# Which queue carries the stores of the first stretch: from SyncE's queue to ScalarE's, and in the last head group to GpSimd's

## The chip, the cores and the metric

The kernel runs on one core of one Trainium2 chip. The metric is device microseconds of the whole program. An engine's name is shortened as in the profile: PE is TensorE (matmuls), DVE VectorE, ACT ScalarE, POOL GpSimd, SP SyncE. A DMA is issued by an instruction in the queue of one of SP, ACT and POOL; this instruction stands in order with the engine's other instructions and waits there until its data are ready. The 16 DMA engines then move the bytes.

## The reference

One inference step of a one-layer hybrid decoder, for a prompt of 512 tokens and for 8 samples of one token each that carry states. Only the first part, a combined projection with two recurrent branches, is touched here:

```python
def layer(x, p, conv_prev, ssm_prev, wkv_prev, shift_prev, lp):
    h = rmsnorm(x, lp['norm_mix'])
    z, xbc_raw, dt_raw, rw_proj, gate_m, gate_r = split_proj(h @ lp['w_in'])
    y_m, conv_new, ssm_new = mamba_branch(z, xbc_raw, dt_raw, ...)
    y_r, wkv_new, shift_new = rwkv_branch(rw_proj, shift_prev, wkv_prev, ...)
    x = x + (jax.nn.sigmoid(gate_m) * y_m + jax.nn.sigmoid(gate_r) * y_r) @ lp['w_out']
    x = x + peer(rmsnorm(x, lp['norm_ffn']), ...)
    x = x + jax.nn.sigmoid(rmsnorm(x, lp['norm_ple']) @ lp['w_ple_gate']) * (p @ lp['w_ple_proj'])

def wkv_scan(r, decay, k, v, a_vec, b_vec, s0):          # RWKV-7, 16 heads of 64
    def step(s, inp):
        rt, wt, kt, vt, at, bt = inp
        s = (s * wt[:, :, None, :]
             + jnp.einsum('bhvk,bhk->bhv', s, at)[..., None] * bt[:, :, None, :]
             + vt[..., None] * kt[:, :, None, :])
        return s, jnp.einsum('bhvk,bhk->bhv', s, rt)
...
    def step(h, inp):                                    # Mamba-2 SSD, 32 heads, in chunks of 128
        st, dec = inp
        return h * dec[..., None, None] + st, h
```

The model width is 1024, everything is fp32. The outputs are the final activations and the new states of prompt and samples.

## The kernel before

The first stretch (about 34 to 1230 us of the span) works through 8 head groups in a loop `for g in range(8)`; a group is two RWKV heads and four SSD heads. Every 128 columns of `w_in` are one projection tile: the weights are loaded by SP's queue (L86, `wraw`, two buffers), split by ACT (L78, `whi`) and DVE (L79, `wlo`) into a high and a low part, and multiplied in three passes (L95, L96, L97), 24 matmuls of 260 columns for each half of the 520 tokens. These matmuls need nothing of the group that is in work, so they can fill PE's time wherever they stand in its order. Below they are called fills.

For a group the steps are: `rwkv_in` (L513 to L567 prepare the chunks' factors), `rwkv_inv` (the inverse of 16x16 blocks: 15 steps on DVE, L598 and L601, an ACT copy L602, then a round trip through DRAM to re-lay the result: a store of `td` L603, a load by ACT's queue L606, then L610 on DVE into `di` and on POOL into `dp`), `rwkv_pre` (PE L513, L645, L655, L665 with DVE L632, L634, L636, L647 and POOL L671), and `rwkv_chain`: 8 dependent steps, each PE L703, DVE L707, PE L711, ACT L712 and L713, PE L717, DVE L723 and L726, and every four of them PE L737 and L735; it ends with PE L743. Then `rwkv_out` (L752 to L762) and `ssd` (L952 to L1019). `gates()` makes the 16 tiles of the two branch gates, each stored by L1065; in the code's order three tiles stand ahead of the last group's chain and 13 behind it.

The 8 samples' recurrent steps run as generators one group behind the prompt: `rwkv_s` (store L814 of five rows to `q5_d`, six broadcast loads L823, the state's load L828, DVE L830 to L836 with POOL L832 and L833, the state's store L837) and `ssd_s` (store L891 to `bc_d`, loads L905 and L906, then twice a state's load L910, POOL L912, DVE L913 and L914, the state's store L915, POOL L916). The last group's own sample steps run beside its chain.

The functions don't fix the order in which an engine takes its instructions. A scheduler at build time picks, from a model of each queue, which of the ready instructions each engine takes next; only those in `pin(...)` keep the order of the code. A changed queue therefore moves other instructions too. Once built, each engine's order is fixed.

Of the kernel before, what the change touches and what calls it, by code (L numbers as in the profile page):

```python
# [18 lines left out]
P = 128  # L19
# [11 lines left out]
def tile_hybrid(ctx: ExitStack, tc, x_prompt, x_sample, p_prompt, p_sample, state_ssm, state_conv,  # L31
# [6 lines left out]
    nc = tc.nc  # L38
    V, S, G, T = nc.vector, nc.scalar, nc.gpsimd, nc.tensor
# [8 lines left out]
    def rowb(ap, n):  # L48
        return ap.unsqueeze(0).to_broadcast([n] + list(ap.shape))
# [20 lines left out]
    bc_d = dram.tile([8, 8, 256], F32, name="bc_d")  # L70
    g_d = dram.tile([2, 8, P, 2, NH], F32, name="g_d")
# [502 lines left out]
    def rwkv_inv(g, ar, bk):  # L574

        L64 = c8(full("de"))
        lc16 = lp.tile([P, 8, 16], F32, name="lw")
        for hf in range(2):
            hs = slice(4 * hf, 4 * hf + 4)
            L = mm4(lambda ro, i: ar[ro, 4 * hf + i, 0, :], lambda ro, i: bk[ro, 4 * hf + i, ro.start // 64, :])  # L580
            V.tensor_tensor(L64[:, hs], L, b64(m64, 4), op=OP.mult)
            lm = c8(full("kk"))[:, 0:4]
            V.tensor_tensor(lm, L, b64(m16, 4), op=OP.mult)
            V.tensor_reduce(lc16[:, hs], lm.rearrange("p c (b k) -> p c k b", k=16), axis=AX.X, op=OP.add)
        ld, td = ld_d[g % 2], td_d[g % 2]
        nc.scalar.dma_start(ld.rearrange("c p k -> p c k"), lc16)
        yield
        lb = lp.tile([64, 16, 16], F32, name="a")
        pin(nc.sync.dma_start(lb.rearrange("q r k -> q (r k)"), ld.rearrange("c (z r) k -> (c z) (r k)", r=16)))
        yield  # L590
        tb = lp.tile([64, 16, 32], F32, name="sq")
        pin(V.memset(tb, 0.0))
        V.memset(tb.rearrange("p r k -> p (r k)")[:, 0:512:33], 1.0)
        tf = lp.tile([64, 16, 16], F32, name="k2")
        for j in range(15):
            tt = tf[:, j + 1:, 0:j + 1]
            sh = [64, 15 - j, j + 1]
            i = V.tensor_tensor(tt, lb[:, j + 1:, j:j + 1].to_broadcast(sh), tb[:, j:j + 1, 0:j + 1].to_broadcast(sh), op=OP.mult)  # L598
            if j == 0:
                pin(i)  # L600
            V.tensor_tensor(tb[:, j + 1:, 0:j + 1], tb[:, j + 1:, 0:j + 1], tt, op=OP.add)  # L601
        S.copy(tb[:, :, 16:32], tb[:, :, 0:16].rearrange("p r k -> p k r"))  # L602
        nc.sync.dma_start(td.rearrange("c (z r) k -> (c z) (r k)", r=16), tb.rearrange("q r k -> q (r k)"))  # L603
        yield
        tc16 = lp.tile([P, 8, 32], F32, name="lw")
        pin(nc.scalar.dma_start(tc16, td.rearrange("c p k -> p c k")))  # L606
        yield
        T16, TT16 = c8(full("di")), c8(full("dp"))
        for q, (E_, t) in enumerate(((V, T16), (G, TT16))):
            pin(E_.tensor_tensor(t.rearrange("p c (b k) -> p c b k", k=16),  # L610
                                 tc16[:, :, None, 16 * q:16 * q + 16].to_broadcast([P, 8, 4, 16]),
                                 mb16[:, None].to_broadcast([P, 8, 4, 16]), op=OP.mult))
        yield L64, T16, TT16
# [135 lines left out]
    def rwkv_out(g, y, bon, lw_):  # L749
# [11 lines left out]
        V.tensor_tensor(y, y, ps, op=OP.mult)  # L761
        nc.sync.dma_start(yr_d[g], y.rearrange("p (i t) -> p i t", i=2))  # L762


    def rwkv_s(g, lw_):
        gs = slice(g * P, (g + 1) * P)
# [44 lines left out]
        T.transpose(ps[:40, 0:P], Q.rearrange("p q b -> p (q b)"), identf)  # L811
        qs = l2.tile([40, P], F32, name="s_qs", bufs=1)
        S.copy(qs, ps[:40, 0:P])
        nc.sync.dma_start(q5_d[g], qs)  # L814
        yield
        sa = t8("sa")

# [2 lines left out]
        qa, qb, qc, w2 = big("sB"), big("sB"), big("sH"), big("sH")  # L820
        for i, (dst, n) in enumerate(((qa, 16), (qb, 16), (qc, 8))):
            for e in range(2):
                m = nc.sync.dma_start(dst[64 * e:64 * e + 64].rearrange("p q b k -> p (q b) k")[:, :n],  # L823
                                      rowb(q5_d[g, 16 * i:16 * i + n, 64 * e:64 * e + 64], 64))
                if i == e == 0:
                    pin(m)
        dec, nkk, bS, kS, rS, sw, t1, t2 = qa[:, 0], qa[:, 1], qb[:, 0], qb[:, 1], qc[:, 0], qc[:, 1], w2[:, 0], w2[:, 1]
        nc.sync.dma_start(sw, state_wkv[0].rearrange("b h v k -> b (h v) k")[:, gs].rearrange("b p k -> p b k"))  # L828
        yield
        pin(V.tensor_tensor(t1, sw, nkk, op=OP.mult))  # L830
        V.tensor_reduce(sa, t1, axis=AX.X, op=OP.add)
# [2 lines left out]
        V.tensor_tensor(t1, bS, bl(sa, 64), op=OP.mult)  # L834
        V.tensor_tensor(sw, sw, t1, op=OP.add)
        V.tensor_tensor(sw, sw, t2, op=OP.add)  # L836
        nc.sync.dma_start(wkv_sample[0].rearrange("b h v k -> b (h v) k")[:, gs].rearrange("b p k -> p b k"), sw)  # L837
        G.tensor_tensor(t2, sw, rS, op=OP.mult)
        V.tensor_reduce(yrS[:, g], t2, axis=AX.X, op=OP.add)

# [32 lines left out]
    def ssd_s(g):  # L873
        def pA():
            return pa.tile([P, 512], F32, name="psA")
        js = (2 * g, 2 * g + 1, 16 + g, 24 + g)
        cvv = cvS.rearrange("p c (b k) -> p c b k", k=3)
        xc = l2.tile([P, 4, 8], F32, name="s_xc", bufs=1)
        th = l2.tile([P, 4, 8], F32, name="s_th", bufs=1)
        for i, j in enumerate(js):  # L880
            V.tensor_scalar(xc[:, i], fl8(xbcS)[:, j], cw[:, 3, j:j + 1], rows["conv_b"][:, j:j + 1], op0=OP.mult, op1=OP.add)
            for k in range(3):
                V.scalar_tensor_tensor(xc[:, i], cvv[:, j, :, k], cw[:, k, j:j + 1], xc[:, i], op0=OP.mult, op1=OP.add)
        S.activation(th, xc, AF.Tanh)
        V.scalar_tensor_tensor(xc, th, 1.0, xc, op0=OP.add, op1=OP.mult)
        ps = pA()
        for i in range(2):
            T.transpose(ps[:8, i * P:(i + 1) * P], xc[:, 2 + i], identf)
        bcs = l2.tile([8, 256], F32, name="s_bc", bufs=1)
        S.copy(bcs, ps[:8, 0:256])  # L890
        nc.sync.dma_start(bc_d[g], bcs)  # L891
        ps = pA()
        for i in range(2):
            for e in range(2):
                T.matmul(ps[64 * e:64 * e + 64, i * 16:i * 16 + 16],
                         lhsT=selb[:, 4 * g + 2 * i + e:4 * g + 2 * i + e + 1].to_broadcast([96, 64]), rhs=limbS, start=True, stop=True)
        dx = l2.tile([P, 2, 16], F32, name="s_dx", bufs=1)
        V.tensor_copy(dx, ps[:, 0:32].rearrange("p (j b) -> p j b", b=16))
        V.tensor_tensor(dx[:, :, 0:8], dx[:, :, 0:8], xc[:, 0:2], op=OP.mult)
        sst = state_ssm[0].rearrange("b h p n -> b (h p) n")  # L900
        sso = ssm_sample[0].rearrange("b h p n -> b (h p) n")
        y2 = yS[:, 2 * g:2 * g + 2]
        yield
        Bb, Cb = (lp.tile([P, 8, P], F32, name="sB", bufs=2) for _ in range(2))
        pin(nc.sync.dma_start(Bb, rowb(bc_d[g, :, 0:P], P)))  # L905
        nc.sync.dma_start(Cb, rowb(bc_d[g, :, P:2 * P], P))  # L906
        for i in range(2):
            rs_ = slice(js[i] * P, (js[i] + 1) * P)
            hs_, t1 = (lp.tile([P, 8, P], F32, name="sH", bufs=2) for _ in range(2))
            pin(nc.sync.dma_start(hs_, sst[:, rs_].rearrange("b p n -> p b n")))  # L910
            yield
            pin(G.tensor_tensor(t1, Bb, bl(dx[:, i, 0:8], P), op=OP.mult))  # L912
            pin(V.tensor_tensor(hs_, hs_, bl(dx[:, i, 8:16], P), op=OP.mult))  # L913
            V.tensor_tensor(hs_, hs_, t1, op=OP.add)  # L914
            nc.sync.dma_start(sso[:, rs_].rearrange("b p n -> p b n"), hs_)  # L915
            G.tensor_tensor(t1, hs_, Cb, op=OP.mult)  # L916
            V.tensor_reduce(y2[:, i], t1, axis=AX.X, op=OP.add)
            if i == 0:
                yield
        for i in range(2):  # L920
            V.scalar_tensor_tensor(y2[:, i], xc[:, i], dsk[:, js[i]:js[i] + 1], y2[:, i], op0=OP.mult, op1=OP.add)
        zs = fl8(zS)[:, 2 * g:2 * g + 2]
        t = l2.tile([P, 2, 8], F32, name="s_t2", bufs=1)
        S.activation(t, zs, AF.Tanh, scale=0.5)
        V.scalar_tensor_tensor(t, t, 1.0, zs, op0=OP.add, op1=OP.mult)
        V.tensor_tensor(y2, y2, t, op=OP.mult)
# [11 lines left out]
    def ssd(g, xt, bm, cm, sz):  # L938
# [59 lines left out]
            T.transpose(ps[:, j * P:(j + 1) * P], st[:, j * P:(j + 1) * P], identf)  # L998
        so = l2.tile([P, 2, P], F32, name="yt")
        S.copy(so, ps[:, 0:256].rearrange("p (j n) -> p j n", j=2))  # L1000
        nc.sync.dma_start(ssm_prompt[0, 0].rearrange("h q n -> (h q) n")[g * 256:(g + 1) * 256].rearrange("(j p) n -> p j n", p=P), so)

        for j in range(2):
            G.tensor_tensor(yf[j], yf[j], sz[j], op=OP.mult)
# [54 lines left out]
    def gates():  # L1059
        for i, c0 in enumerate((W_GR, W_GM)):  # L1060
            for o in range(8):
                ps = proj(c0 + o * P, P, hT)
                gt = l2.tile([P, 2, NH], F32, name="dtmp")
                S.activation(gt, ps[:, :, :NH], AF.Tanh, scale=0.5)
                nc.sync.dma_start(g_d[i, o], gt)  # L1065
                step()
                yield
    gates_ = gates()
# [644 lines left out]
```

## Time and profile before

| | us |
|---|---|
| median of 3 runs | 3083.57 (3078.41 to 3088.08) |
| the profiled execution's own time | 3087.78 |
| its span, from the first to the last instruction | 3086.1 |
| PE busy | 2819.7 (91%) |
| DVE busy | 2268.4 (74%) |
| ACT busy | 988.0 (32%) |
| POOL busy | 679.2 (22%) |
| mean granted PE clock | 0.944 of full speed |

The rows of the next sections come from the profiled execution; start times are microseconds from the beginning of its span. It is 4.2 us (0.14%) longer than the median run. The span holds the first stretch to about 1230 us, the output projections and keys to about 1580 us, and the PEER passes and the end behind them.

### The profile page before, as it was taken

How to read it: one execution, taken by the hardware profiler on the slowest of the kernel's cores; microseconds unless marked ns; L12 is line 12 of the kernel's file. 1: busy time of each engine (PE TensorE's matmuls, PEld its weight loads, DVE VectorE, ACT ScalarE, POOL GpSimd, SP SyncE). 2: the span in 40 equal slices, each digit the busy share in tenths (PEclk: the TensorE clock that was granted, in tenths of full speed). 3: DMA queues.
4: the chain of work that ended last, by engine and by line, in shares of the span. 5: the costliest groups of instructions: out<-in, count | busy, mean ns of one | idle time of the engine just before them, and what ended most of it. 6: DMA issues, size and time to landing. Idle time of an engine off the chain costs nothing. (4 is left out here: it accounts for less than half of the span.)

```text
span 3086.1 us, 52530 instructions
## 1 busy us (share of the span) xinstructions
PE 2819.7 (91%) x20187; PEld 2617.2 (85%) x20192; DVE 2268.4 (74%) x5375; ACT 988.0 (32%) x1995; POOL 679.2 (22%) x508
## 2 busy tenths in 40 slices
PE   5999989898897988998987989898999999999998
PEld 4878878787776878896976989898999999999996
DVE  5768787877777684435899999695677777877846
ACT  2333333333241322322222324233222343333322
POOL 0222131212313121210003132121222323432300
PEclk8999999898988898999998999999999999999999
DMA  3214242433324264633224767677898888999830
GB/s 92 71 41 105 78 114 57 105 62 100 82 69 107 61 139 145 203 98 129 76 75 156 240 216 235 218 245 234 299 330 310 321 300 311 332 327 321 290 124 28
DMA packets 459091, 528.15 MB, mean 171 GB/s; under 512 B 102632, under 2 KB 370555, under 8 KB 458801
## 3 DMA queue, kind: packets, MB, share of 16 engines
q1 hardware_dynamic: 405337, 388.99, 41.4%
q0 software_dynamic: 36864, 134.23, 12.6%
q10 hardware_dynamic: 16640, 1.57, 0.4%
q8 instruction: 159, 2.61, 0.4%
q14 instruction: 91, 0.75, 0.1%
HBM read 447.83 MB, written 77.14 MB: 170 GB/s over the span
## 5 line engine op out<-in xcount | busy, mean ns | idle before, releaser
L96 PE MATMUL ps<-hlo,whi 128*128 128x260 f32 (+1 forms) x1456 | 444.0, 305 | 0.0
L97 PE MATMUL ps<-hhi,wlo 128*128 128x260 f32 (+1 forms) x1456 | 443.1, 304 | 0.1
L95 PE MATMUL ps<-hhi,whi 128*128 128x260 f32 (+1 forms) x1456 | 442.2, 304 | 0.3 <-ACT hhi L155 0.3
L97 PE MATMUL psA<-h2h,ul 128*128 128x392 f32 x1024 | 352.9, 345 | 27.4 <-DVE ul L1496 26.9
L95 PE MATMUL psA<-h2h,uh 128*128 128x392 f32 x1024 | 364.2, 356 | 0.2 <-ACT uh L1495 0.2
L95 PE MATMUL av<-ah,vh 128*128 128x392 f32 x1024 | 349.9, 342 | 3.8 <-ACT vh L78 3.2
L96 PE MATMUL psA<-h2l,uh 128*128 128x392 f32 x1024 | 353.3, 345 | 0.0
L97 PE MATMUL av<-ah,vl 128*128 128x392 f32 x1024 | 351.8, 344 | 1.3 <-DVE vl L79 1.3
L96 PE MATMUL av<-al,vh 128*128 128x392 f32 x1024 | 350.5, 342 | 2.3 <-DVE al L79 2.3
L97 PEld LDWEIGHTS ps<-hhi,wlo 128*128 128x128 f32 (+1 forms) x1456 | 286.4, 197 | 11.9 <-issue 5.9
L95 PEld LDWEIGHTS ps<-hhi,whi 128*128 128x128 f32 (+1 forms) x1456 | 286.3, 197 | 12.0 <-issue 5.5
L96 PEld LDWEIGHTS ps<-hlo,whi 128*128 128x128 f32 (+1 forms) x1456 | 286.9, 197 | 10.3 <-issue 4.4
L1449 POOL DMA_INDIRECT gr<-in_peer_v_dram,e x128 | 194.8, 1522 | 363.8 <-DVE o L1464 346.4
L1449 POOL DMA_INDIRECT gr<-in_peer_u_dram,e x128 | 127.4, 995 | 498.1 <-DVE junk L1458 452.1
L78 ACT CAST vh<-vr 128x1024 fp32r<-128x1024 f32 x128 | 134.3, 1051 | 315.8 <-PE av L96 155.1
L97 PEld LDWEIGHTS psA<-h2h,ul 128*128 128x128 f32 x1024 | 195.7, 191 | 30.9 <-DVE ul L1496 29.7
L78 ACT CAST whi<-wraw 128x1024 fp32r<-128x1024 f32 (+1 forms) x115 | 119.9, 1042 | 313.8 <-PE ps L96 247.9
L95 PEld LDWEIGHTS av<-ah,vh 128*128 128x128 f32 x1024 | 193.5, 189 | 4.8 <-ACT vh L78 3.5
L95 PEld LDWEIGHTS psA<-h2h,uh 128*128 128x128 f32 x1024 | 195.6, 191 | 0.9 <-ACT uh L1495 0.9
L96 PEld LDWEIGHTS psA<-h2l,uh 128*128 128x128 f32 x1024 | 196.3, 192 | 0.0
L96 PEld LDWEIGHTS av<-al,vh 128*128 128x128 f32 x1024 | 193.2, 189 | 3.1 <-DVE al L79 3.1
L97 PEld LDWEIGHTS av<-ah,vl 128*128 128x128 f32 x1024 | 193.2, 189 | 1.8 <-DVE vl L79 1.8
(627 smaller groups left out, 6453.0 us busy)
## 6 DMA issues: line engine op xcount, KB each, us to landing
ur<-in_peer_u_dram SPq DMA_DIRECT2D x128, 512.0 KB
vr<-in_peer_v_dram SPq DMA_DIRECT2D x128, 512.0 KB
wraw<-in_w_in_dram SPq DMA_DIRECT2D x90, 512.0 KB
Gt<-G_d SPq DMA_DIRECT2D x32, 784.0 KB
G_d<-stg SPq DMA_DIRECT2D x12, 2048.0 KB
ge_d<-ge SPq DMA_DIRECT2D x112, 196.0 KB
gl<-ge_d SPq DMA_DIRECT2D x112, 196.0 KB
sB<-q_d SPq DMA_DIRECT2D x32, 256.0 KB
```

Source lines behind the costliest of these rows:

```text
L78: S.copy(hi, raw)
L95: T.matmul(out, lhsT=a[0], rhs=b[0], start=start, stop=False)
L96: T.matmul(out, lhsT=a[0], rhs=b[1], start=False, stop=False)
L97: T.matmul(out, lhsT=a[1], rhs=b[0], start=False, stop=stop)
L1449: pin(G.indirect_dma_start(out=t, out_offset=None, in_=(peer_u, peer_v)[s_ // P][0], in_offset=bass.IndirectOffsetOnAxis(ap=e3[:, s_ % P:s ...
```

## The change

Two groups of DMA instructions are issued by another engine; what they move, and where the code stands, is the same.

- In all groups, the stores of what ACT made are issued by ACT and no longer by SP: L603 (`td`), L814 (`q5_d`), L891 (`bc_d`), L1001 (the prompt's SSD state, an output) once in each of 8 groups, and L1065 (`g_d`) 16 times, 48 DMAs.
- A helper `Qu(g)` gives POOL's queue for the last group (g == 7) and SP's otherwise. Through it go the samples' loads and state stores: six L823, L828, L837, L905, L906, two L910 and two L915, so 14 DMAs of the last group are issued by POOL.

```diff
-        nc.sync.dma_start(td.rearrange("c (z r) k -> (c z) (r k)", r=16), tb.rearrange("q r k -> q (r k)"))
+        nc.scalar.dma_start(td.rearrange("c (z r) k -> (c z) (r k)", r=16), tb.rearrange("q r k -> q (r k)"))
...
+    def Qu(g):
+
+        return G if g == 7 else nc.sync
+
...
-        nc.sync.dma_start(q5_d[g], qs)
+        nc.scalar.dma_start(q5_d[g], qs)
...
-                m = nc.sync.dma_start(dst[64 * e:64 * e + 64].rearrange("p q b k -> p (q b) k")[:, :n],
+                m = Qu(g).dma_start(dst[64 * e:64 * e + 64].rearrange("p q b k -> p (q b) k")[:, :n],
...
-        nc.sync.dma_start(sw, state_wkv[0].rearrange("b h v k -> b (h v) k")[:, gs].rearrange("b p k -> p b k"))
+        Qu(g).dma_start(sw, state_wkv[0].rearrange("b h v k -> b (h v) k")[:, gs].rearrange("b p k -> p b k"))
...
-        nc.sync.dma_start(wkv_sample[0].rearrange("b h v k -> b (h v) k")[:, gs].rearrange("b p k -> p b k"), sw)
+        Qu(g).dma_start(wkv_sample[0].rearrange("b h v k -> b (h v) k")[:, gs].rearrange("b p k -> p b k"), sw)
...
-        nc.sync.dma_start(bc_d[g], bcs)
+        nc.scalar.dma_start(bc_d[g], bcs)
...
-        pin(nc.sync.dma_start(Bb, rowb(bc_d[g, :, 0:P], P)))
-        nc.sync.dma_start(Cb, rowb(bc_d[g, :, P:2 * P], P))
+        pin(Qu(g).dma_start(Bb, rowb(bc_d[g, :, 0:P], P)))
+        Qu(g).dma_start(Cb, rowb(bc_d[g, :, P:2 * P], P))
...
-            pin(nc.sync.dma_start(hs_, sst[:, rs_].rearrange("b p n -> p b n")))
+            pin(Qu(g).dma_start(hs_, sst[:, rs_].rearrange("b p n -> p b n")))
...
-            nc.sync.dma_start(sso[:, rs_].rearrange("b p n -> p b n"), hs_)
+            Qu(g).dma_start(sso[:, rs_].rearrange("b p n -> p b n"), hs_)
...
-        nc.sync.dma_start(ssm_prompt[0, 0].rearrange("h q n -> (h q) n")[g * 256:(g + 1) * 256].rearrange("(j p) n -> p j n", p=P), so)
+        nc.scalar.dma_start(ssm_prompt[0, 0].rearrange("h q n -> (h q) n")[g * 256:(g + 1) * 256].rearrange("(j p) n -> p j n", p=P), so)
...
-                nc.sync.dma_start(g_d[i, o], gt)
+                nc.scalar.dma_start(g_d[i, o], gt)
```

The helper takes four lines, so in the changed kernel each line behind it has a number that is 4 higher: L823 is L827, L830 is L834, L836 is L840, L912 is L916, L916 is L920, and L913 is L917; all text here uses the numbers of before.

The scheduler's order changes with the queues. On PE, this is the second half of the last group's chain before the change (`uv`, `X`, `TT` and `ctok` are the chain's own tiles, x2 the two heads):

```order
L737 MATMUL psB<-AM,uv 64x64 x8
L735 MATMUL psB<-ar,st 64x64 x8
L703 MATMUL psB<-uv,AM 64x64 x2
L711 MATMUL psB<-X,TT_11985 64x64 x2
L717 MATMUL psB<-uv,ctok 64x64 x2
L703 MATMUL psB<-uv,AM 64x64 x2
L711 MATMUL psB<-X,TT_11985 64x64 x2
L717 MATMUL psB<-uv,ctok 64x64 x2
```

The same place on PE after the change (`hhi`, `hlo` are the activations' parts, `whi`, `wlo` the weights' of a gate or projection tile):

```order
L703 MATMUL psB<-uv,AM 64x64 x2
L97 MATMUL ps<-hhi,wlo 128x260
L95 MATMUL ps<-hhi,whi 128x260
L96 MATMUL ps<-hlo,whi 128x260
L97 MATMUL ps<-hhi,wlo 128x260
L95 MATMUL ps<-hhi,whi 128x260
L96 MATMUL ps<-hlo,whi 128x260
L97 MATMUL ps<-hhi,wlo 128x260
L95 MATMUL ps<-hhi,whi 128x260
L711 MATMUL psB<-X,TT_11985 64x64 x2
L96 MATMUL ps<-hlo,whi 128x260
```

Counted over the whole order, the last group's chain (L701 to L743) holds no fill before and 125 after; from L743 to L760 it is 39 and 63, and from there to the end of the gates (PE L845) 345 and 168. 28 fills of the 384 stand ahead of the chain now. In groups 1 to 6 the chain holds 125 to 148 fills before, and 97 to 158 after.

On POOL, this is the last group before the change (L912 and L916 ahead of L671 belong to group 6's samples, all behind to group 7's):

```order
L916 TENSOR_TENSOR sH<-sH,sB 128x1024
L671 COPY AM<-ar 64x4x64 x2
L833 TENSOR_TENSOR sH<-sB,s_x_11923 128x512
L832 TENSOR_TENSOR sH<-sH,sB 128x512
L838 TENSOR_TENSOR sH<-sH 128x512
L912 TENSOR_TENSOR sH<-sB,s_dx 128x1024
```

The same place on POOL after it:

```order
L827 DMA sB<-q_d 64x16x64 x2
L920 TENSOR_TENSOR sH<-sH,sB 128x1024
L671 COPY AM<-ar 64x4x64 x2
L827 DMA sB<-q_d 64x16x64
L671 COPY AM<-ar 64x4x64 x2
L827 DMA sB<-q_d 64x16x64
L827 DMA sH<-q_d 64x8x64 x2
L832 DMA sH<-in_state_wkv_dram 128x8x64
L837 TENSOR_TENSOR sH<-sB,s_x_11923 128x512
L836 TENSOR_TENSOR sH<-sH,sB 128x512
L841 DMA out_dram<-sH 128x8x64
L842 TENSOR_TENSOR sH<-sH 128x512
```

Seven DMAs now stand between POOL's own operations here (the rows x2 count twice, and the first two are ahead of group 6's last L916); the other seven follow behind.

On DVE, this is group 5 before the change, from the samples' state update to the first evictions of `rwkv_pre`; the inverse's last step L601 stands 7 rows ahead of the first row shown:

```order
L836 TENSOR_TENSOR sH<-sH 128x512
L775 TENSOR_TENSOR s_x_9774<-s_x_9774,rwS 128x24
L792 TENSOR_SCALAR s_kx<-s_x_9774,VB 128x8
L804 COPY s_Q<-s_x_9774 128x8
L793 TENSOR_TENSOR s_t<-s_kx 128x8
L839 TENSOR_REDUCE yrS<-sH 128x8
L610 TENSOR_TENSOR di<-lw,mb_270 128x512
L632 TENSOR_TENSOR bb<-psB,di 128x256
L913 TENSOR_TENSOR sH<-sH,s_dx 128x1024
L632 TENSOR_TENSOR a<-psB,di 128x256
```

The same group on DVE after the change, first from the inverse's last step on:

```order
L601 TENSOR_TENSOR sq<-sq,k_8442 64x15
L79 TENSOR_TENSOR wlo<-wraw,whi 128x1024
L610 TENSOR_TENSOR di<-lw,mb_270 128x512
L834 TENSOR_TENSOR sH<-sH,sB 128x512
L835 TENSOR_REDUCE s_sa<-sH 128x8
L838 TENSOR_TENSOR sH<-sB,s_sa 128x512
```

and then, some rows on, around the evictions:

```order
L843 TENSOR_REDUCE yrS<-sH 128x8
L632 TENSOR_TENSOR bb<-psB,di 128x256
L632 TENSOR_TENSOR a<-psB,di 128x256
L634 TENSOR_TENSOR k_8791<-psB,di 128x256
L634 TENSOR_TENSOR sq<-psB,di 128x256
L917 TENSOR_TENSOR sH<-sH,s_dx 128x1024
```

L610 has moved from behind the samples' operations to ahead of them, and L913 from between the two L632 to behind the four evictions; groups 4 and 6 read alike, and L610 has moved so in groups 1, 2 and 7 too (in group 3 it stands behind L830). POOL's L610 keeps its place there, behind the samples' L832, L833 and L838.

## Rows read from the trace of the kernel before

**Rows 1.** Windows: stretch in us, its length, each engine's busy us, PE clock, DMA share, GB/s.

```profile
core 0: us, PE busy (x) PEld busy (x) DVE busy (x) ACT busy (x) POOL busy (x), PEclk, DMA share, GB/s
305.20:335.95 30.75, 30.75 (x318) 25.78 (x316) 20.21 (x58) 11.40 (x33) 7.81 (x5) 1.00 0.35 100
...
1149.81:1177.31 27.50, 15.66 (x170) 10.86 (x170) 15.55 (x57) 6.30 (x24) 3.23 (x5) 0.50 0.50 103
1177.31:1188.07 10.76, 10.28 (x70) 8.39 (x67) 4.86 (x17) 1.26 (x3) 3.16 (x2) 0.87 0.73 200
1188.07:1230.00 41.93, 41.93 (x349) 41.69 (x347) 18.39 (x21) 10.87 (x15) 8.26 (x3) 1.00 0.60 177
34.00:1240.00 1206.00, 1069.92 (x9383) 933.92 (x9388) 885.28 (x2181) 383.96 (x976) 278.52 (x206) 0.90 0.36 89
```

**Rows 2.** The same windows, PE's instructions of L95 alone.

```profile
305.20:335.95 30.75, 13.02 (x43) 8.09 (x43) 1.00 0.35 100
...
1149.81:1177.31 27.50, 0.00 (x0) 0.00 (x0) 0.50 0.50 103
...
1188.07:1230.00 41.93, 32.88 (x115) 21.63 (x115) 1.00 0.60 177
```

**Rows 3.** Timeline of PE in the last group's chain: start, us, instruction, [idle before it <-releaser].

```profile
1168.90 0.48 PE L717 MATMUL psB<-uv,ctok 128*64 128x64 f32 x4 [0.54 <-ACT uv L713]
```

**Rows 4.** Timeline of PE where the gates end.

```profile
1229.90 0.33 PE L845 MATMUL psB<-yrS,bdm 128*128 128x64 f32 x2
```

**Rows 5.** Timeline of DVE where the last group's sample steps end.

```profile
1209.65 0.29 DVE L867 TENSOR_TENSOR yS<-yS,VB 128x128 f32<-128x128 f32 x1
```

**Rows 6.** Waits of PE, 70 to 1240 us: us in total, times, longest.

```profile
PE psB L513 <- POOL dp L610: 17.4, 5, 6.1
```

**Rows 7.** Waits of ACT in the same window.

```profile
ACT whi L78 <- PE ps L96: 174.5, 57, 13.0
```

**Rows 8.** Waits of SP's queue in the same window.

```profile
SPq L603 <- ACT sq L602: 43.1, 7, 7.8
```

**Rows 9.** Groups by line: ns min/median/max of one issue, first and last start.

```profile
L603 SPq DMA_DIRECT2D td_d<-sq x8: 477/484/484, 146.9 to 1111.5; - x8
L814 SPq DMA_DIRECT2D q_d<-s_qs x8: 295/304/313, 257.5 to 1131.6; - x8
L891 SPq DMA_DIRECT2D bc_d<-s_bc x8: 286/298/432, 253.1 to 1161.1; - x8
L1001 SPq DMA_DIRECT2D out_dram<-yt x8: 383/389/1502, 190.2 to 1132.0; - x8
L1065 SPq DMA_DIRECT2D g_d<-dtmp x16: 319/332/532, 1058.5 to 1231.6; - x16
...
L823 SPq DMA_DIRECT2D sB<-q_d x32: 590/934/2524, 259.1 to 1150.7; - x32
...
L1449 POOL DMA_INDIRECT gr<-in_peer_u_dram,e x128: 932/936/1926, 1637.6 to 2348.3; - x128
```

**Rows 10.** Timeline of POOL in the last group.

```profile
1157.02 1.04 POOL L833 TENSOR_TENSOR sH<-sB,s_x 128x512 f32<-128x512 f32 x1 [6.23 <-DMA sB<-q_d]
1174.02 1.26 POOL L832 TENSOR_TENSOR sH<-sH,sB 128x512 f32<-128x512 f32 x1 [15.95 <-DVE sH L830]
```

**Rows 11.** Timeline of SP's queue in the last group.

```profile
1151.62 2.13 SPq L823 DMA_DIRECT2D sH<-q_d  x2
```

**Rows 12.** Timeline of DVE in group 5, behind the inverse.

```profile
834.00 0.68 DVE L830 TENSOR_TENSOR sH<-sH,sB 128x512 f32<-128x512 f32 x1
...
842.19 0.67 DVE L610 TENSOR_TENSOR di<-lw,mb 128x512 f32<-128x512 f32 x1
...
848.81 1.23 DVE L913 TENSOR_TENSOR sH<-sH,s_dx 128x1024 f32<-128x1024 f32 x1 [3.81 <-DMA sH<-in_state_ssm_dram]
```

**Rows 13.** Timeline of POOL in group 5.

```profile
840.39 1.26 POOL L610 TENSOR_TENSOR dp<-lw,mb 128x512 f32<-128x512 f32 x1
```

**Rows 14.** Timeline of PE in group 5, from the inverse to the chain's inputs.

```profile
841.70 1.97 PE L513 MATMUL psB<-dp,de 64*64 64x64 f32 x32 [6.07 <-POOL dp L610]
...
850.42 1.12 PE L513 MATMUL psB<-a 64*64 64x64 f32 x16 [4.39 <-DVE a L632]
...
856.01 2.40 PE L645 MATMUL psB<-ar,bk 64*128 64x128 f32 x16 [2.15 <-DVE TT L636]
```

## The prediction, made before the changed kernel ran

> **What bounds the kernel now.** First the windows over the first stretch: of its 1206 us PE is busy 1069.92, at a mean clock of 0.90, so here the time goes where PE stands idle or runs at the lower of its two levels [rows 1]. The change leaves the order on all engines alone behind the gates, so only this stretch counts. Then the windows of single chains. The chain of group 1 took 30.75 us with PE busy throughout, at full clock, with 43 matmuls of L95, about 129 fills. That of the last group took 27.50 us with none, PE busy 15.66 us at half clock; its 345 fills stand behind it and took 41.93 us, PE busy throughout [rows 1, 2]. The timeline shows why the empty chain is slow: PE waits for ACT and DVE in each step, here 0.54 us ahead of L717 [rows 3]. So the last group pays twice, 11.84 us idle and a half clock, then fills on their own at 41.93/345 = 0.1215 us each. The gates end at 1229.90, the samples' last step at about 1210 [rows 4, 5]: 20 us of slack on the sample side.
>
> Then the lists of waits: is SP, which is relieved, a bound? ACT's cast of a weight tile waits 174.5 us in total for PE to free its buffer [rows 7], so weights lie there early. And SP waits for ACT's copy ahead of L603 in 7 of 8 groups [rows 8], so the store leaves the moment its data are there. A store on ACT can't leave earlier. What could gain, then, isn't the queue itself but the order that the scheduler makes with it.
>
> **The change part by part.**
>
> *48 stores to ACT.* By the medians 8 x 0.484 + 8 x 0.304 + 8 x 0.298 + 8 x 0.389 + 16 x 0.332 = 17.1 us more work for ACT [rows 9]. ACT is busy 383.96 of 1206 us [rows 1], and most stores stand behind the ACT operation that made the data, not ahead of one for which PE waits. Cover is missing in the last chain only, where five of them fall between L712 and L713 of its steps: 5 x 0.33 = 1.6 us. Without cover anywhere it would be 17.1; I take 1.6.
>
> *The last group's order on PE.* Before: 27.50 + 10.76 + 41.93 = 80.2 us from L703's first step to the gates' end [rows 1]. After: the chain holds 125 fills, like group 1's. It takes 30.75 less 4 x 0.12, and 1.6 for ACT's stores, so 31.9. The stretch to L760 has 24 fills more, 10.76 + 24 x 0.1215 = 13.7. The 168 left take 20.4. Together 66.0, so 14.2 less. 28 fills have moved ahead of the chain, where they cost between nothing (if PE waits there anyway) and 28 x 0.1215 = 3.4; I take 2. This term is -12. Bounds: -14 where all of it holds; 0 where the chain stalls at the same places in spite of fills.
>
> *14 DMAs to POOL.* How long POOL is held by issuing a broadcast DMA of 64 partitions is in no row. SP takes 0.934 us for one [rows 9]. POOL's own gathers of 128 rows take 0.932 [rows 9], and L823 has 64 x 16 = 1,024 runs, eight times as many: 0.93 and 8 x 0.93 = 7.4 us are the two ends. I take 1.5 us, near the lower end, since nothing in the rows shows a price per run, and SP's price for the same DMA lies there. What waits behind them: two stand ahead of L916 and four between L671 and L833. POOL starts these four at about 1151, so the load of the state leaves at 1151 + 4t; from SP's last L823 (1151.62) to L833's start was 5.4 us [rows 10, 11]. DVE's L830 then stands ready at 1156.4 + 4t, and in the new order it is ahead of the fifth chain step's L723. That step comes at about 1166 (half of the chain). So up to t = 2.4 it costs nothing; beyond, the whole chain waits 4 us for each us of t. Four more DMAs (L837, L905, L906, the first L910) stand ahead of L913, which stands ahead of part of `rwkv_out` on DVE: again 4 us for each us, from about the same t. So nothing up to t = 2, then 8 us per us. At 1.5 nothing. What POOL computes there took 3.23 us in the chain [rows 1], so it has room. At the end, the samples finish near 1212 at t = 2, the gates at about 1218, so this path is hidden too, but only by some 6 us.
>
> A sentence by the Trainium skill on the same price: "DMA: Bandwidth & Descriptors", section "Anatomy of one DMA — SWDGE (gpsimd) path", states that descriptor generation on this path is small and variable, and that many descriptors can be emitted before it shows; by that t stays near the low end and the sum is the same -12. No run here shows it so far.
>
> *Groups 1 to 6 on DVE.* The sum could fail here. In group 5 the inverse's end was at 834.0; the samples' L830 and its kin ran while the block made its way through DRAM, and DVE's L610 came at 842.19, POOL's at 840.39, right behind POOL's L838 [rows 12, 13]. PE waited 6.07 us for that `dp` [rows 14]; in all groups such waits came to 17.4 us [rows 6]. In the new order DVE's L610 is ahead of the sample operations. It waits for the round trip, at most to 840.4 (POOL's L610 had its data then), and they run behind it. POOL's L610 still stands behind POOL's L838, which needs DVE's L836. So the chain of sample operations, 834.00 to the end of POOL's L610 at 841.65, 7.65 long, starts up to 7 us later: `dp` comes late by 0 (if the round trip is short) to 7 us. I take 5, in groups 4 to 6 and in one of the earlier ones (there, fills have covered such waits so far). On the other side, L913 no longer stands between the two L632. It waited 3.81 us for its state's load, and through it PE waited 4.39 for `a` and then 2.15 for TT [rows 12, 14]; that is 6.5 us per group, in groups 4 to 6. So 4 x 5 - 3 x 6.5 = about 0. Bounds: -20 (no delay, the stalls gone) to +28 (four groups by 7, nothing given back).
>
> **Sum**: -12 + 0 = -12; against the profiled execution (3087.78, span 3086.1) about 3076, against the median of 3083.57, which is 0.14% lower, 3071.6; I say 3071. The forecast's own range is 3058 to 3077, from a few us of middle groups given back or lost.
>
> **The rivals.**
>
> *The middle groups eat it.* `dp` is late by 5 in four groups and the stalls on L632 don't fall away, since DVE is late by as much as L913 was. Then -12 + 20 = +8: 3091; with half of that, 3081. For it: these stalls are in the trace, on PE, with nothing beside them. Against: the evictions come ahead of L913 now, as they did in groups 1 to 3, where PE did not wait so long.
>
> *GpSimd's queue is slow* (the other side). The mechanism: POOL, held t per DMA, feeds L830 and L913 late, and the last chain stands behind them on DVE. It outweighs the 12 us from t = 3.5, is 0.3% slower from t = 4.7, and at 7.4 gives -12 + 43 = +31: 3115. For it: 1,024 runs against the gather's 128 rows. Against: SP issues the same in 0.9.
>
> *The change does nothing.* If a fill only moves from one place to another and the chain's waits stay (each fill delays the chain's next matmul by what it hid), the time is 3083. For it: the fills behind the chain ran dense already. Against: group 1's chain, dense at 30.75 us with 129 fills, where 129 fills alone cost 15.7, so it does overlap. The Trainium skill's "DMA: Bandwidth & Descriptors", section "Issuing engines are not separate DMA queues", speaks for this rival: DMAs of all issuers interleave on the same 16 engines, and issuing on several saves the sequencer's time alone. By that the moved DMAs themselves gain nothing, which agrees with the waits on SP, and it would be 3083 too; the order of PE isn't in the rule.
>
> **How the numbers follow.** 0.3% of the time, 9.25 us, is about what a measurement of this kernel can tell from no change: below 3074.3 is faster, above 3092.8 slower. The forecast has 0.50 (0.47 of it faster), the middle groups 0.23 (0.18 same, 0.05 slower), slow POOL 0.19 (0.14 slower, 0.03 same, 0.02 still faster by its small end), no effect 0.08. So faster 0.49, same 0.32, slower 0.19. The likeliest is 3071. The range of 3050 to 3102 takes in the forecast with the middle groups' gain down to -20 in part, the second and fourth case whole, and slow POOL up to t of about 6; what is left out is 0.05 below and 0.08 above. The forecast's own range, 3058 to 3077, stands beside it since both signs are held.
>
> **What the new profile would show.** Right: in the last chain's window some 42 matmuls of L95, PE busy nearly throughout at a clock near 1.0, some 32 us from L703's first step to L743, and the gates ending about 66 us behind the chain's start. Each DMA row on POOL at 0.9 to 2 us. The waits of PE for `dp` longer than 17.4 us in total, those for `a` at L632 shorter. Wrong: a wait of DVE's L830 or L913 for their loads in the last group, with PE's L703 behind it (POOL slow); PE waits for `dp` of 10 us or more per group with the ones behind it unchanged (middle groups); or a last chain that holds its fills and still lasts 27.5 + 15 us (no effect).

## The result, and the profile after

The changed kernel takes 3057.57 us (median of 6 runs, 3051.57 to 3070.37), the kernel before, beside it, 3087.35 (3078.41 to 3098.93). The ratio is 0.9891, with a 95% interval of 0.9873 to 0.9908: 1.1% or about 34 us faster. The forecast was 12 us and the median lies outside the range of the forecast's own case (3058 to 3077) by a hair; the wide range, 3050 to 3102, holds it, but the gain is nearly three times the one forecast.

In the profiled execution (span 3049.9) the gates end at 1199.78 where they ended at 1229.90 [rows 4], 30.1 us earlier. About half of that lies in the last group, from its chain's start to the gates' end: 80.1 us before, 64.9 now. The other half is gone ahead of it: the last chain starts at 1134.84, where it started at 1149.81. The span is 36.2 us shorter; the other 6 us lie behind the gates, where no order changed, and runs of one kernel differ by more than that. The windows of the last chain and of what is behind it, in the columns of [rows 1]:

```profile
1134.84:1163.41 28.57, 28.44 (x297) 23.25 (x294) 17.65 (x51) 10.04 (x28) 8.33 (x9) 1.00 0.47 119
1163.41:1199.78 36.37, 34.03 (x258) 32.03 (x258) 21.90 (x32) 7.26 (x11) 11.39 (x7) 0.95 0.61 183
34.00:1210.00 1176.00, 1071.33 (x9383) 933.45 (x9387) 864.21 (x2181) 384.92 (x977) 296.83 (x220) 0.92 0.36 91
```

The same chain, PE's instructions of L95 alone, as in [rows 2]:

```profile
1134.84:1163.41 28.57, 12.10 (x41) 7.71 (x41) 1.00 0.47 119
```

The chain took about as long as the empty one (28.57 against 27.50), at full clock and with PE busy throughout, and holds 41 of L95; what is behind it is 16 us shorter. That is the fill that the order showed. Over the stretch to 10 us behind the gates, PE's idle time was 1206 - 1069.92 = 136.1 us before [rows 1] and is 1176 - 1071.33 = 104.7 now, at the same busy time. The equal busy time is a balance of two parts. These are the windows of groups 1 to 3 and of groups 4 to 6, each from a group's first L513 to another's, before:

```profile
229.93:653.34 423.41, 386.30 (x3461) 333.55 (x3464) 336.25 (x803) 150.11 (x391) 105.59 (x78) 0.95 0.36 87
653.34:1075.05 421.71, 364.72 (x3130) 318.47 (x3130) 309.00 (x749) 128.47 (x329) 97.03 (x74) 0.86 0.35 85
```

and after:

```profile
226.07:654.36 428.29, 400.58 (x3462) 344.66 (x3463) 322.58 (x803) 149.67 (x391) 104.60 (x78) 0.93 0.35 86
654.36:1052.87 398.51, 351.30 (x3115) 306.60 (x3115) 297.49 (x747) 129.43 (x329) 105.81 (x73) 0.89 0.36 88
```

Groups 1 to 3 are 4.9 us longer: 9.4 us less idle, but 14.3 more busy, at a lower mean clock (0.93 against 0.95). Groups 4 to 6 are 23.2 us shorter, 9.8 of it idle time and 13.4 busy time, at a higher mean clock (0.89 against 0.86).

The waits of PE, 70 to 1240 us, for the lines of [rows 6]:

```profile
PE psB L513 <- POOL dp L610: 23.2, 6, 6.7
...
PE psB L645 <- DVE TT L636: 3.3, 6, 0.8
...
PE psB L513 <- DVE a L632: 0.2, 1, 0.2
```

The waits for `dp` have grown, from 17.4 to 23.2. Those for `a` at L632 are down to 0.2. In the kernel before, the same list from 600 to 1012 us (groups 4 to 6) had them so:

```profile
PE psB L513 <- POOL dp L610: 16.2, 3, 6.1
PE psB L513 <- DVE a L632: 12.6, 3, 4.4
...
PE psB L645 <- DVE TT L636: 6.4, 3, 2.1
```

Group 5 in the timeline of PE after, from the inverse to the chain's start; the rows answer to [rows 14]:

```profile
837.97 1.97 PE L513 MATMUL psB<-dp,de 64*64 64x64 f32 x32 [6.69 <-POOL dp L610]
...
845.24 1.16 PE L645 MATMUL psB<-ar,bk 64*128 64x128 f32 x8 [0.79 <-DVE TT L636]
...
856.25 0.42 PE L701 MATMUL psB<-uv,AM 64*64 64x64 f32 x4
```

And DVE there, as [rows 12], from the inverse's last step L601 on (L913 is now numbered L917):

```profile
822.06 0.16 DVE L601 TENSOR_TENSOR sq<-sq,k 64x15 f32<-64x15 f32 x1
...
829.68 0.69 DVE L610 TENSOR_TENSOR di<-lw,mb 128x512 f32<-128x512 f32 x1
...
841.70 0.42 DVE L632 TENSOR_TENSOR a<-psB,di 128x256 f32<-128x256 f32 x1 [0.43 <-PE psB L513]
...
843.63 1.22 DVE L917 TENSOR_TENSOR sH<-sH,s_dx 128x1024 f32<-128x1024 f32 x1
```

From `dp`'s L513 to the first L645 it is now 7.3 us, before 14.3 [rows 14]: the state update waits for nothing and stands ahead of none of the four evictions; PE waits 0.79 for the TT behind it. POOL's L610 there, as [rows 13]:

```profile
836.66 1.26 POOL L610 TENSOR_TENSOR dp<-lw,mb 128x512 f32<-128x512 f32 x1
```

And the whole stretch of group 5 from `dp`'s L513 to the chain's start, first before, then after:

```profile
841.70:869.85 28.15, 19.79 (x218) 17.73 (x219) 18.82 (x23) 7.40 (x16) 10.03 (x8) 0.56 0.68 193
837.97:856.25 18.28, 14.71 (x209) 13.22 (x210) 14.22 (x19) 5.44 (x11) 10.01 (x6) 0.69 0.80 225
```

It is 9.9 us shorter: 4.8 of idle time and 5.1 of busy time. Nine fills that stood in it before, 0.22 us apart where fills at full clock are 0.12 apart, are no longer in it (218 matmuls against 209).

POOL's DMAs, as groups by line (L827 is L823 of before):

```profile
L827 POOL DMA_DIRECT2D sB<-q_d x4: 820/852/1071, 1119.5 to 1132.9; - x4
L827 POOL DMA_DIRECT2D sH<-q_d x2: 694/699/704, 1133.7 to 1134.4; - x2
```

0.7 to 1.1 us each, under the 1.5 that the forecast took. The samples' last step on DVE, as [rows 5], comes 7 us ahead of the gates' end:

```profile
1192.78 0.29 DVE L871 TENSOR_TENSOR yS<-yS,VB 128x128 f32<-128x128 f32 x1
```

### The profile page after: what moved, and what is told of

The parts are those of the page before. It is cut to its first block, busy times and chain, and to the rows that moved or that the text cites. A ratio compares the mean times of both kernels' runs of the same rounds, so it can differ in the third digit from the quotient of the medians.

```text
span 3049.9 us, 52517 instructions
## 1 busy us (share of the span) xinstructions
PE 2821.5 (93%) x20188; PEld 2617.4 (86%) x20192; DVE 2249.9 (74%) x5375; ACT 988.6 (32%) x1995; POOL 685.8 (22%) x522
## 2 busy tenths in 40 slices
DMA packets 446995, 528.15 MB, mean 173 GB/s; under 512 B 95464, under 2 KB 357243, under 8 KB 446705
## 5 line engine op out<-in xcount | busy, mean ns | idle before, releaser
L95 PE MATMUL ps<-hhi,whi 128*128 128x260 f32 (+1 forms) x1456 | 443.8, 305 | 0.6 <-DVE rsa L122 0.3
L95 PE MATMUL psA<-h2h,uh 128*128 128x392 f32 x1024 | 365.7, 357 | 0.2 <-ACT uh L1499 0.2
L95 PE MATMUL av<-ah,vh 128*128 128x392 f32 x1024 | 348.9, 341 | 3.3 <-ACT vh L78 3.2
L95 PEld LDWEIGHTS ps<-hhi,whi 128*128 128x128 f32 (+1 forms) x1456 | 286.6, 197 | 13.9 <-issue 6.8
L97 PEld LDWEIGHTS ps<-hhi,wlo 128*128 128x128 f32 (+1 forms) x1456 | 286.3, 197 | 12.6 <-issue 4.0
L1453 POOL DMA_INDIRECT gr<-in_peer_v_dram,e x128 | 184.3, 1440 | 367.9 <-DVE o L1468 349.7
L95 PEld LDWEIGHTS psA<-h2h,uh 128*128 128x128 f32 x1024 | 196.7, 192 | 0.9 <-ACT uh L1499 0.9
L79 DVE TENSOR_TENSOR vl<-vr,vh 128x1024 fp32r<-128x1024 f32 x128 | 156.2, 1222 | 55.4 <-ACT vh L78 52.2
L95 PEld LDWEIGHTS av<-ah,vh 128*128 128x128 f32 x1024 | 192.9, 188 | 3.9 <-ACT vh L78 3.5
```

The source lines that it names most:

```text
L79: eng.tensor_tensor(lo, raw, f(hi), op=OP.subtract)
L95: T.matmul(out, lhsT=a[0], rhs=b[0], start=start, stop=False)
L97: T.matmul(out, lhsT=a[1], rhs=b[0], start=False, stop=stop)
L1453: pin(G.indirect_dma_start(out=t, out_offset=None, in_=(peer_u, peer_v)[s_ // P][0], in_offset=bass.IndirectOffsetOnAxis(ap=e3[:, s_ % P:s ...
```

## The experiments

Two theories stood at the start. One: only the order that the scheduler builds matters, and there are two separate gains, the last chain's fill and the place of L913 and L610 in the middle groups. Rival: SP's queue is relieved, and the gain goes with the DMAs taken off it. All ratios are to the kernel before, run beside.

**Only the gates' stores on ACT** (L1065):

```diff
-                nc.sync.dma_start(g_d[i, o], gt)
+                nc.scalar.dma_start(g_d[i, o], gt)
```

> Only the 16 stores of the gates (L1065) are issued by ACT; everything else as before. In the built order groups 0 to 6 are as before, and the last group's chain holds 127 fills in place of none. Theory (order on PE in the last group, and order in groups 1 to 6, as two separate gains): the last group alone gains, about 15 us, so some 3072 where before is 3087; the chain's window runs at a clock near 1.0 with some 42 of L95, and the waits of PE at L513, L632, L636 in groups 4 to 6 stay. Rival (what gains is SP's relief, in proportion to the DMAs taken off it): 16 of 62, so about 8 us of 30.

Measured: 3082.23, ratio 0.9962 (0.9947 to 0.9977), about 12 us. The last chain's window:

```profile
1160.38:1188.67 28.29, 28.29 (x300) 23.45 (x297) 17.66 (x51) 9.87 (x27) 3.96 (x4) 1.00 0.55 142
```

So the last group's fill alone, without any other change, is worth the 12 us that the forecast gave it. By the share of DMAs it would be 8 or 9; this run doesn't separate the two.

**Only the td store on ACT** (L603, 8 DMAs):

```diff
-        nc.sync.dma_start(td.rearrange("c (z r) k -> (c z) (r k)", r=16), tb.rearrange("q r k -> q (r k)"))
+        nc.scalar.dma_start(td.rearrange("c (z r) k -> (c z) (r k)", r=16), tb.rearrange("q r k -> q (r k)"))
```

> Only the 8 stores of td (L603) are issued by ACT. In the built order groups 1 to 6 change as in the full change (DVE's L610 ahead of the samples' L836, L913 behind the four evictions), and the last chain holds 8 fills, so stays nearly empty. Theory of two gains: the middle groups alone gain, about 15 us, so some 3072; groups 4 to 6 are each about 7 us shorter, and the last chain and what is behind it stay at about 80 us. Rival (SP's relief in proportion): 8 of 62, about 4 us.

Measured: 3066.25, ratio 0.9914 (0.9894 to 0.9934), about 27 us: the middle groups alone, since the last chain is as slow as before:

```profile
1132.16:1160.08 27.92, 17.84 (x178) 12.67 (x178) 13.15 (x47) 6.11 (x23) 2.98 (x3) 0.50 0.32 77
```

Eight DMAs bring twice what sixteen bring in the run before; the gain doesn't go with their number.

**All 48 stores on ACT, the last group's 14 DMAs left on SP** (the change without `Qu`):

> All 48 stores on ACT, the 14 DMAs of the last group stay on SP. In the built order the middle groups are exactly as in the full change and the last chain holds 129 fills. Theory of two gains: both are there, so the time is that of the full change, 3058, within 0.3%, and GpSimd's queue is worth nothing. Rival (GpSimd's queue gains by itself in the last group): 5 to 10 us slower than the full change.

Measured: 3056.54, ratio 0.9877 (0.9855 to 0.9898), the time of the full change within the interval, and the sum of the two runs above (0.38% + 0.86% against 1.23%). GpSimd's queue adds nothing.

**Only the last group's 14 DMAs on GpSimd** (`Qu` alone):

> Only the 14 DMAs of the last group go to GpSimd's queue, no store moves to ACT. In the built order groups 0 to 6 are as before and the last chain holds 130 fills. Theory of two gains: as with the gates' stores alone, about 15 us less, some 3072, the DMAs on POOL at 0.9 us each delaying nothing. Rival (SP's relief in proportion): 14 of 62, about 7 us; rival (POOL's DMAs hold the sample steps up): less than that or a loss.

Measured: 3081.36, ratio 0.9959 (0.9942 to 0.9976). By itself it fills the last chain as the gates' stores do, with the same gain, about 13 us; together with them there is nothing left to fill.

**No queue changed, only the five stores' priority raised**:

```diff
-        nc.sync.dma_start(q5_d[g], qs)
+        with tc.high_priority(600): nc.sync.dma_start(q5_d[g], qs)
...
-                nc.sync.dma_start(g_d[i, o], gt)
+                with tc.high_priority(600): nc.sync.dma_start(g_d[i, o], gt)
```

(and so L603, L891 and L1001.)

> No queue changes: all DMAs stay on SP and ACT as before. Only the scheduler's priority of the five stores (L603, L814, L891, L1001, L1065) is raised, which makes it build nearly the order of the change: in groups 1 to 6 L913 behind the four evictions, 0 fills in rwkv_pre of groups 4 to 6, and 124 fills in the last chain. Theory (the built order alone makes the gain): about as fast as the full change, 3055 to 3065 where before is 3090. Rival (SP's queue was late, and taking stores off it is the gain): within 5 us of before.

Measured: 3048.76, ratio 0.9853 (0.9836 to 0.9870), about 45 us: faster than the change (the intervals of the two ratios don't meet), and with every store on SP as before. An order alone, without any other queue, makes the whole gain. In groups 4 to 6 its order has L610 behind the samples' L836, as before, and L913 behind the evictions, as after; the list of PE's waits from 600 to 1000 us:

```profile
PE psB L513 <- POOL dp L610: 12.3, 3, 4.1
...
PE psB L645 <- DVE TT L636: 4.6, 4, 1.8
```

The waits for `a` are gone here too, and `dp` is waited for 4.1 us a group, less than in group 5 before [rows 14] or after. So L913's place goes with the gain and L610's place doesn't. L610's place goes with the delay: from the inverse's end to the end of POOL's L610 it is 9.1 to 9.2 us in groups 4 to 6 here, and 15.7 to 18.6 in the change, where DVE has L610 ahead of the samples' L830. But the nine fills are out of `rwkv_pre` here too, so this run doesn't tell L913's place from theirs.

**24 stores on ACT with the order nearly kept** (L814, L891 and L1001; L603 and L1065 on SP):

> 24 of the 48 stores on ACT (L814, L891, L1001), L603 and L1065 left on SP. The built order stays nearly that of before: L610 and L913 where they were in all groups, 9 fills in rwkv_pre of groups 4 to 6, 15 fills in the last chain in place of none. Theory (only the order gains, the queues do nothing): within 0.3% of before, 0 to 3 us less. Rival (SP's relief gains): half of the stores, so 10 to 15 us less.

Measured: 3094.34, ratio 1.0002 (0.9985 to 1.0018): nothing. Of its PE waits from 600 to 1012 us those for `a` are as before (12.6), those for `dp` less (16.2 before):

```profile
PE psB L513 <- DVE a L632: 12.4, 3, 5.2
PE psB L513 <- POOL dp L610: 12.3, 3, 4.1
```

Together with the run above it this speaks against the rival: order without queues gains all, and half of the queues' move, with the order nearly kept, gains none.

**The priority of the td store alone** (L603 as above, still on SP):

> No queue changes; only the priority of L603 is raised. In the built order L913 is behind the four evictions in groups 1 to 6, L610 is ahead of the samples' L836 in groups 1, 3 and 4 only, and the last chain holds no fill. Theory of two gains: the middle gain alone, with L603 still on SP, 25 to 35 us. Rival (moving L603 to ACT's queue is part of the gain): under 15 us.

Measured: 3070.14, ratio 0.9925 (0.9901 to 0.9950), about 23 us, a little under the 25 that was expected, with an interval that takes in the td store on ACT. The middle gain needs no other queue either.

**The state update left out of groups 3 to 5**, to price L913:

```diff
-            pin(V.tensor_tensor(hs_, hs_, bl(dx[:, i, 8:16], P), op=OP.mult))
-            V.tensor_tensor(hs_, hs_, t1, op=OP.add)
+            if g not in (3, 4, 5): pin(V.tensor_tensor(hs_, hs_, bl(dx[:, i, 8:16], P), op=OP.mult))
+            if g not in (3, 4, 5): V.tensor_tensor(hs_, hs_, t1, op=OP.add)
```

> As before, but DVE leaves out the samples' SSD state update (L913 and L914) of groups 3, 4 and 5, which stand between the evictions in groups 4 to 6; the sample outputs of these groups are then not the reference's. POOL's L912 and L916 and all DMAs remain. Theory (L913, waiting for its state's load, holds up the evictions and through them PE): in groups 4 to 6 the waits for `a` at L632 (12.6 us in sum) and TT at L636 (6.4) vanish, the 6 us wait for dp in each stays, and each group is 7 to 10 us shorter, so 20 to 30 us in all. Rival (the middle gain is from L610 coming ahead of the samples' operations): the four evictions are not what costs, so under 8 us in all, since L610 is still behind.

Measured: 3086.68, ratio 0.9976 (0.9959 to 0.9992), 7 us: as the rival had it. But the timeline of DVE in group 5 shows that the wait was not taken away:

```profile
855.87 0.43 DVE L632 TENSOR_TENSOR a<-psB,di 128x256 f32<-128x256 f32 x1 [0.43 <-PE psB L513]
858.46 1.22 DVE L917 TENSOR_REDUCE yS<-sH 128x8 f32<-128x1024 f32 x1 [2.16 <-POOL sH L916]
859.60 0.41 DVE L634 TENSOR_TENSOR k<-psB,di 128x256 f32<-128x256 f32 x1
```

The sum L917 had moved into L913's place; it waits for POOL's L916, which waits for the same load, and PE waits for `k` behind it instead of `a`, in the list from 600 to 1012 us:

```profile
PE psB L513 <- DVE k L634: 12.1, 3, 6.8
```

In groups 5 and 6 of this run the nine fills are out of `rwkv_pre`, so 7 us is what their place and four operations of DVE less a group bring while the stall stays. A further run leaves out L917 too:

```diff
-            V.tensor_reduce(y2[:, i], t1, axis=AX.X, op=OP.add)
+            V.tensor_reduce(y2[:, i], t1, axis=AX.X, op=OP.add) if g not in (3, 4, 5) else V.memset(y2[:, i], 0.0)
```

> As before, but DVE leaves out L913, L914 and L917 (the sum that waited in L913's place in the run before) of the samples' SSD step in groups 3, 4 and 5, whose sample outputs are then wrong. Nothing of the samples' SSD step stands between the evictions in groups 4 to 6. Theory (an operation between the evictions that waits for its state's load costs the middle groups): the waits of PE at L632, L634 and L636 in groups 4 to 6 shrink from 19 us to under 5, and each of these groups is about 7 us shorter, 15 to 25 us in all. Rival (the middle gain is elsewhere): under 8 us, as in the run before.

Measured: 3073.53, ratio 0.9946 (0.9928 to 0.9964), about 17 us, within what the theory gave. Of the waits for L632, L634 and L636 one is left in the list from 600 to 1000 us:

```profile
PE psB L645 <- DVE TT L636: 4.8, 1, 4.8
```

The edit differs from the run before by L917 alone, and the ratio by 0.30%, about 9 us, which is the stall between the evictions and two operations of 1.2 us a group. Of the middle groups' 23 to 27 us the 17 are an upper bound for the stall, since the fills' place and DVE's six operations a group are in them too.

**L603 and L1065 on ACT, nothing else:**

> L603 and L1065 on ACT, nothing else moved. In the built order groups 4 to 6 are those of the td store alone and the last chain holds 128 fills. Theory of two gains: their sum, 27 + 12 = 39 us, about 3050 where before is 3090; as fast as all 48 stores on ACT or a few us faster, since the td block is back after 2.3 us (4 to 5 with all stores moved). Rival (the gains overlap): 30 us or less.

Measured: 3057.87, ratio 0.9884 (0.9865 to 0.9903), about 36 us: the sum, 1.24%, lies in the interval. It is not faster than all stores on ACT.

**The same, with dp's L610 on DVE:**

```diff
-        for q, (E_, t) in enumerate(((V, T16), (G, TT16))):
+        for q, (E_, t) in enumerate(((V, T16), (V, TT16))):
```

> As the td and gate stores on ACT, and in addition the second L610 (dp) is made by DVE and no longer by POOL, where it stood behind the samples' L838. Theory (PE's wait for dp, 5 to 6 us in each of groups 4 to 6 and 25 us in sum, comes from POOL's order): most of it goes, 12 to 18 us less than without this edit. Rival (DVE's evictions or L610 on DVE become the next wait): no change or a loss, with the waits of PE moved to L632 or L636.

Measured: 3057.03, ratio 0.9891 (0.9873 to 0.9910), no change. The wait for `dp` stays, and another thing ends it; DVE and PE in group 5:

```profile
822.91 0.69 DVE L610 TENSOR_TENSOR di<-lw,mb 128x512 f32<-128x512 f32 x1 [2.09 <-DMA lw<-td_d]
...
824.86 1.97 PE L513 MATMUL psB<-dp,de 64*64 64x64 f32 x32 [6.60 <-DVE dp L610]
```

L610 waits for the load of the block itself. From the inverse's end to the end of `dp` it is 8.3 us here in group 5, and 10.5 in the run before it; the 2 us do not show in the time.

## Why the prediction was wrong, step by step

**Right: the queues themselves.** That a store on ACT leaves no earlier and SP is no bound was read from the waits [rows 7, 8]; 24 moved stores with the order nearly kept changed nothing (1.0002).

**Right: the last group.** Forecast -12; the two runs that have it alone gave 12 and 13 us. The sum of 66.0 us from the chain's start to the gates' end was 64.9. What the forecast took off for work moved ahead was put too small: 2 us, and in group 7, from the first L513 to the chain's start, the change takes 7.2 us longer than before (82.0 against 74.8), so that in its own profile the last group as a whole gives 8 us.

**Right: GpSimd.** 1.5 us per DMA was taken, 0.7 to 1.1 measured, under the 2 us from which it would cost; with and without it the time is the same.

**Wrong: the middle groups.** The step is "So 4 x 5 - 3 x 6.5 = about 0", taken as the sum over groups 1 to 6. The td store alone, with the last chain empty, measured -27. By the windows above, groups 1 to 3 lost 4.9 us in the change, about the 5 put for one of the earlier groups. Groups 4 to 6 gained 23.2 where the step has 3 x 5 - 3 x 6.5 = -4.5: there both terms were off, and on the same side.

The loss: the delay came, and was larger than the 5 taken. From the inverse's end to the end of POOL's L610 group 5 took 7.65 us before (834.0 to 841.65) and takes 15.7 now (822.22 to 837.92). But it did not reach PE: the waits for `dp` grew by 5.8 us in all [rows 6], and by 2.6 in groups 4 to 6 (16.2 to 18.8), not by 15. I had moved `dp` and left PE where it was. In group 5, from its first L513 (797.59 before, 789.15 after) to where it began to wait for `dp` (its start less its wait, [rows 14]), PE's own stream is now 42.1 us long, before 38.0, as matmuls of `ssd` (L961 to L973) and 12 more fills stand in it, and counted from that L513 the inverse ends 3.4 us earlier; the two cover nearly all of the delay.

The gain: from `dp`'s L513 to the chain's start group 5 took 28.2 us before and takes 18.3 now, 9.9 less where 6.5 was put (groups 4 and 6 are 9.0 and 9.7 shorter). I counted the two stalls that [rows 14] shows. Left out were the nine fills at the lower clock behind them, and the clock of the matmuls that stay: its mean over this stretch was 0.56 before and is 0.69 now.

Over groups 1 to 6 the change's profile is 18.3 us shorter. That lies close to the bound of -20, but not by its condition, "no delay, the stalls gone": the delay was there and hidden, and more than the stalls went. One reading beside it was also wrong: in groups 1 to 3 before, three of the four evictions stood ahead of L913, not all.

The run with raised priorities shows the two terms apart: with L913 behind the evictions, the fills out of `rwkv_pre` and L610 not ahead, the middle groups gain and `dp` is waited for less. Which part of the gain is L913's stall and which the fills' place is known only by the bounds of the two runs that leave out work.

**Not settled:** why the run with raised priorities is 10 us faster than the change. By the same windows its groups 1 to 3 took 417.4 us and its groups 4 to 6 391.2, where the change has 428.3 and 398.5. The largest single piece is group 2 from `dp`'s L513 to the chain's start, first with raised priorities, then in the change:

```profile
424.46:441.38 16.92, 15.27 (x238) 13.33 (x238) 14.05 (x26) 4.62 (x10) 6.47 (x7) 1.00 0.58 153
414.94:443.32 28.38, 27.89 (x242) 24.30 (x244) 15.45 (x31) 5.66 (x14) 9.86 (x9) 0.52 0.35 94
```

PE is busy in both, at full clock in one and at 0.52 in the other. With raised priorities DVE's L610 stands behind the samples' L830 in groups 1 to 6, in the change ahead of it in five of them; that this is the cause is not shown, since L610's place was not tried alone. The move of L603 and L1065 to ACT with the order of before was not tried either; the other three stores stand for it.

## What to carry to other kernels

Where a scheduler sets the order, a changed queue is first of all a changed order: compare the built orders on each engine, then ask whether the gain can be had by priority alone. When a producer is moved later, move the consumer's own stream too before pricing the wait. And price a stall by the whole stretch to the next fixed point, here from `dp` to the chain, with its clock and the other work that stands in it, not by the waits listed at its first lines.

## What the hardware showed that I had not expected

The block's trip through DRAM took longer where the DMA engines were carrying other loads. The store of td was followed by the issue of its load after 2.28 us in group 5 before (SP's store at 834.82, ACT's load at 837.10 in the timelines), after 2.26 with the td store alone on ACT, and after 4.06 in the full change:

```profile
822.94 0.46 ACTq L603 DMA_DIRECT2D td_d<-sq  x1
827.00 0.37 ACTq L606 DMA_DIRECT2D lw<-td_d  x1
```

There, SP had issued the samples' six broadcast loads from 816.91 to 822.5. The DMA view from 820 to 830 us, in slices of 0.25 us (digits as in the page's slices), has the engines full until 826:

```profile
DMA  9999999999999999999999993000000069920000
```

In the kernel before, they stood empty from 831.75 to 835.75, so the store of 834.82 had them to itself (the same view, 831 to 841). No run changed those loads alone:

```profile
DMA  9920000000000000000289100000299700008899
```

Also, the last group's 14 DMAs were far fewer packets on GpSimd's queue than on SP's. The lists of queues of before and of after:

```profile
q1 hardware_dynamic: 405337, 388.99, 41.4%
q0 software_dynamic: 36864, 134.23, 12.6%
```

```profile
q1 hardware_dynamic: 386153, 377.42, 40.1%
q0 software_dynamic: 38304, 139.22, 13.5%
```

On GpSimd's queue (q0) that is 1,440 packets for 4.99 MB, 3.5 KB each, for DMAs whose rows in the kernel's layout are 256 or 512 B. With these 14 DMAs alone moved, q1 fell from 405,337 packets to 391,801, so there they had been 13,536. In all, the program's packets fell from 459,091 to 446,995 while its bytes stayed the same.
